# Scatter-add of node features over edges: new places for the steps of the second sort, and one-hots in halves only up to slot 5

## The chip, the cores and the metric

One core of a Trainium2 chip. The metric is device time in microseconds of one execution of the whole program. Three executions of the kernel before were timed, and one more was profiled.

## What is computed

`reference()` adds, for each of 65,536 edges, the 128 features of the source node to the row of the destination node. There are 4,096 nodes, and the edges are drawn at random.

```python
output = np.zeros((num_nodes, dim), dtype=np.float32)
for i in range(len(edge_index_src)):
    output[edge_index_dst[i]] += node_features[edge_index_src[i]]
```

## The kernel before

The features are held as 32 source blocks of 128 rows, and the output is made as 32 destination buckets of 128 nodes. The edges are sorted by destination bucket (the first sort, up to about 50 us), and then, for each of 8 groups of four buckets, by source block (the second sort). What is left is dense work on TensorE (PE): for a source block and a destination bucket, a one-hot of the source rows times a one-hot of the destination columns, both with the edges along the partitions, gives a 128x128 matrix of edge counts (`blocks`, L840, into the PSUM tile `psa`). ScalarE (ACT) copies it to `a`, and `product` (L847) multiplies the block's features by it and adds to `pso`, which holds 512 destinations. Each feature matrix is multiplied in two parts, a rounded one and its remainder.

The main loop (L920) has 32 slots, four for each group, with 8 source blocks in each. For a slot s VectorE (DVE) makes the one-hots of slot s+1 (`onehots`, L825, two instructions of 128x4096 when whole, four of 128x2048 when in halves), and PE does the following: `blocks` of k = 0 to 3 of slot s (16 matmuls), the second half of the products of slot s-1 (8 matmuls), `blocks` of k = 4 to 7 (16), and the first half of the products of slot s (8). The one-hots lie in two buffers, so those of slot s+2 wait for the last `blocks` of slot s. Below, "slot s starts" is the time of the first `psa` matmul of slot s.

The second sort of a group g (`pass2`, L643) has to be done before the one-hots of slot 4g. It is a chain over all engines, and each step is hooked into a place of the loop, written `at(slot, where, step)`. In the order of the code, where 0 is ahead of the one-hots, 1 is right behind them, 2 is ahead of the products of the slot before, 3 and 4 are behind the last `blocks`, and 5 is at the end of the slot. Since the schedule is manual, each engine runs its instructions in exactly the order in which the hooks issue them. The steps are:

- `buckets` (DVE, L662, writes `oh2`), then `chunk_sums` (POOL, L677, writes `two2`, `four2`)
- `payloads` of the group before (POOL, L671, writes `v2`)
- `before_all` (three PE matmuls into `psb`, then ACT writes `base2`, L688), then `masked` and `folded` (POOL, L718 and L724, on `cum2`)
- `repeats` (DVE, L698: a copy and two comparisons into `same2`), then `repeats_folded` (POOL, L713)
- `ranks` (eight PE matmuls into `psr2`, which read `cum2` and `same2`; ACT copies them to `rank2`, L732)
- `permutations` (two instructions of DVE into `p2a` or `p2c`, L745)
- `permuted` (48 PE matmuls into `ps2`, which read `v2`; ACT takes them to `pairs`, L748), then `quad_keys` (two of ACT, L761), which the one-hots of slot 4g read

`two2`, `four2` and `same2` have one buffer each, `oh2`, `cum2` and `v2` two, in turn for even and odd groups. Finished groups go out through `evacuate` (ACT) and `finish` (DVE transpose, L415, then DMAs of the SP queue).

Of the kernel before, what the change touches and what calls it, by code (L numbers as in the profile page):

```python
# [28 lines left out]
GROUPS = (4,) * 8  # L29
WARM = 38  # L30
LATE_PAYLOADS = (2, 3, 4, 5, 6)

TURN = 10
WIN = ((0, 5, 0, 44), (5, TURN, 0, 76), (TURN, 15, 48, 124), (15, NJ, 72, P))
# [45 lines left out]
def _fast(ctx, tc, X, src32, dst32, out, ident, fmax, flag_i, T):  # L80
# [20 lines left out]
    for a, b in runs:  # L101
        at, n = 8 * sum(QN[:a]), 4 * QN[a]
# [152 lines left out]
    def onehot(dst, keys2, n, m=P, io=None, m0=0):  # L255

        io = (piota if io is None else io)[:, None, m0:m0 + m].to_broadcast([P, n, m])
        V.tensor_tensor(  # L258
            out=dst.rearrange("p i (m k) -> p i m k", k=2),
            in0=io.rearrange("p i (m k) -> p i m k", k=2),  # L260
            in1=keys2[:, :, None, :].to_broadcast([P, n, m // 2, 2]), op=OP.is_equal)
# [269 lines left out]
    def pair_onehot(t, r, cs):  # L531
        onehot(t[:, cs].rearrange("p c (u m) -> p (c u) m", u=2)[:, :, :WIDE2],
               r[:, cs].rearrange("p c u k -> p (c u) k"), 2 * (cs.stop - cs.start), WIDE2)
# [13 lines left out]
    def take_pairs(pa, x):  # L547

        x = x.rearrange("p (a j s u) -> p a j s u", a=2, j=2, u=2)
        d = pa.rearrange("p (s j a) -> p a j s", j=2, a=2)  # L550
        S.copy(out=d[:64], in_=x[:64, :, :, :, 0])
        for a in range(2):
            S.copy(out=d[64:, 1 - a], in_=x[64:, a, :, :, 1])
# [9 lines left out]
    def pairs_tile():  # L563
        return sb1.tile([P, 4 * NB], BF16, name="pairs", tag="iota4")
# [68 lines left out]
    owed = {}  # L633
    hooks = {}

    def at(slot, where, *fs):
        hooks.setdefault((slot, where), []).extend(fs)
# [5 lines left out]
    def pass2(g):  # L643
# [101 lines left out]
        def permutations(j):  # L745
            pair_onehot(p2b[d0 // 2 % 4 + j], T2["r"][:, j], slice(0, NCH))

        def permuted(j):  # L748
            if j == 0:
                T2["ps2"] = ps.tile([P, 512], F32, name="ps2", tag="ps2", bufs=1)  # L750
            ps2 = T2["ps2"]
            for c in range(NCH):
                at = (c // NH * 2 + j) * 64
                PE.matmul(out=ps2[:, at:at + 64], lhsT=p2b[d0 // 2 % 4 + j][:, c, :],  # L754
                          rhs=T2["v"][:, c, :, 2 * j:2 * j + 2],
                          start=c % NH == 0, stop=c % NH == NH - 1)
            if j == 1:
                T2["k"] = pairs_tile()
                take_pairs(T2["k"][:], ps2[:, :8 * NB])
# [33 lines left out]
            return lambda: [f() for f in fs]  # L793

        if g == 1:
            at(1, 2, ranks, lambda: permutations(0), lambda: permutations(1))
            at(2, 3, lambda: permuted(0), lambda: permuted(1))
            at(2, 4, quad_keys)
            return buckets, payloads, column_sums, sums_to_each, counts
        if g == 2:  # L800
            owed[2] = payloads
            at(1, 5, before_all, masked, folded)
            at(2, 1, repeats, repeats_folded)
            at(4, 5, ranks)
            at(5, 1, lambda: permutations(0), lambda: permutations(1))
            at(6, 3, lambda: permuted(0), lambda: permuted(1))
            at(6, 5, quad_keys)
            return buckets, chunk_sums
        f = 4 * g
        at(*{3: (3, 1), 4: (6, 1)}.get(g, (f - 11, 4)), buckets, chunk_sums,  # L810
           owed.pop(g - 1, lambda: None))
        after_sums = (5, 5) if g == 3 else (f - 7, 3 if g < 6 else 2)
        at(*after_sums, before_all, masked, folded)
        if g in LATE_PAYLOADS:
            owed[g] = payloads
        else:
            at(*after_sums, payloads)
        at(*((6, 1) if g == 3 else after_sums), repeats, repeats_folded)
        at(f - 4, 3, ranks)
        at(f - 3, 1, lambda: permutations(0), lambda: permutations(1))  # L820
        moves, keys = {3: ((10, 3), (10, 5)), 4: ((14, 2), (14, 5))}.get(g, ((f - 3, 5), (f - 2, 2)))
        at(*moves, lambda: permuted(0), lambda: permuted(1))
        at(*keys, quad_keys)

    def onehots(slot):  # L825

        oh = sb1.tile([P, 2, 4 * 8, P], BF16, name="oh", tag=f"t2{slot % 2}")
        at = slot % 4 * 32
        parts = ((0, 16), (16, 16)) if slot < 9 else ((0, 32),)
        for i, n in ((0, 4), (4, 4), (8, 8), (16, 16)) if slot == 0 else parts:  # L830
            if i == 8 and slot == 0:
                sums_1()
            for k, io in ((0, piota), (1, piotad)):
                onehot(oh[:, k, i:i + n], keys2[slot // 4][k][:, at + i:at + i + n], n, io=io)
        if slot == 0:
            buckets_2()
            chunk_sums_2()
        return oh
# [29 lines left out]
    def flag_of_all(fall):  # L868
# [3 lines left out]
                               op=OP.not_equal)  # L872

    buckets_1, payloads_1, column_sums_1, sums_1, counts_1 = pass2(1)
    buckets_2, chunk_sums_2 = pass2(2)
    for g in range(3, len(GROUPS)):
        pass2(g)
# [37 lines left out]
    counting_1 = counts_1()  # L915
    next(counting_1)
    oh = onehots(0)
    slots = NB
    prev, pso = None, None
    for slot in range(slots):  # L920
        do(slot, 0)
        cur = oh
        if slot + 1 < slots:
            oh = onehots(slot + 1)
# [130 lines left out]
```

## Time and profile before

| what | us |
| --- | --- |
| timed executions | 264.77, 263.05, 264.54 |
| their median | 264.54 |
| profiled execution, device time | 263.02 |
| its span from the first to the last instruction | 261.4 |
| PE busy | 247.2 (95% of the span) |
| DVE busy | 232.5 (89%) |
| ACT busy | 197.0 (75%) |
| POOL busy | 196.8 (75%) |
| mean granted TensorE clock | 0.995 of full speed |

The slices of the page show DVE at 9 tenths and POOL at 9 tenths through most of the first four fifths, and POOL idle from about 209 us on. In the chain of work that ended last PE has 63% and DVE 24%. Times in the rows below are us from the start of the span, and a row with x16 merges 16 instructions; in rows of the timeline the bracket at the end is idle time of that engine before the row and what ended it. Two successive PE rows can overlap by some 0.16 us, since matmuls are pipelined.

### The profile page before, as it was taken

The numbers are of one execution on the slowest core, as the hardware profiler recorded it, in microseconds if no ns is written. First come the engines' busy times: TensorE is split into PE (matmuls) and PEld (weight loads), VectorE is DVE, ScalarE is ACT, GpSimd is POOL, SyncE is SP. The second block draws the span as 40 slices with busy tenths as digits, with TensorE's granted clock in tenths as the row PEclk, the third lists the DMA queues.
The fourth block names the chain that finished last, engine by engine and source line by source line (L and its number), as shares of the span: only waits on it lengthen the run. The fifth ranks groups of instructions, "written<-read, shape, count | busy, mean of one in ns | idle before, by whom it ended". The sixth has DMA issues, their size and how long they took to land.

```text
span 261.4 us, 7518 instructions
## 1 busy us (share of the span) xinstructions
PE 247.2 (95%) x3155; PEld 208.3 (80%) x3156; DVE 232.5 (89%) x245; ACT 197.0 (75%) x455; POOL 196.8 (75%) x211
## 2 busy tenths in 40 slices
PE   7899999899999999899599999999999999999991
PEld 7689999768887888687488877888888888888780
DVE  6998878999999999999999999999999889789701
ACT  5799997698987786678388687687859776887660
POOL 6399999999999999999994999999999900000000
PEclk9999999999999999999999999999999999999998
DMA  5900000000000000220002001100200020002002
GB/s 161 317 8 8 3 4 5 3 0 3 4 0 4 0 3 0 43 40 3 0 0 43 4 1 19 24 3 0 42 1 3 0 44 0 3 1 43 0 1 44
DMA packets 19140, 5.75 MB, mean 22 GB/s; under 512 B 17056, under 2 KB 18592, under 8 KB 19104
## 3 DMA queue, kind: packets, MB, share of 16 engines
q1 hardware_dynamic: 17232, 4.59, 8.0%
q10 hardware_dynamic: 1872, 0.66, 1.2%
q8 instruction: 25, 0.41, 0.6%
q14 instruction: 11, 0.09, 0.1%
HBM read 3.15 MB, written 2.10 MB: 20 GB/s over the span
## 4 chain that ended last, share of the span: by engine, by line
PE 63%; DVE 24%; POOL 4%; issue 4%; ACT 2%; POOLq 0%; DVEq 0%
PE pso L850 33%; DVE oh L258 19%; PE psa L843 16%; PE psm L388 3%; POOL v L363 2%; PE ps L754 2%; PE psc L302 2%; POOL vc L483 2%; PE psw L152 2%; ACT cum L307 1%; DVE p2a L258 1%; DVE p2c L258 1%; PE psc L304 1%; PE pst L280 1%; PE psr L321 1%
## 5 line engine op out<-in xcount | busy, mean ns | idle before, releaser
L845 ACT CAST a<-psa 128x512 fp32r<-128x512 f32 x256 | 131.9, 606 | 36.1 <-PE psa L843 36.0
L850 PE MATMUL pso<-a,xr 128*128 128x512 f32 x512 | 134.0, 404 | 0.0
L850 PEld LDWEIGHTS pso<-a,xr 128*128 128x128 f32 x512 | 91.4, 189 | 16.7
L258 DVE TENSOR_TENSOR oh<-psi,slo 128x4096 bf16<-128x4096 uint16 (+3 forms) x43 | 74.4, 1731 | 3.0 <-PE psa L843 2.1
L258 DVE TENSOR_TENSOR oh<-psi,dlo 128x4096 bf16<-128x4096 uint16 (+3 forms) x43 | 74.5, 1732 | 0.0
L843 PEld LDWEIGHTS <-oh 128*128 128x128 bf16 x1024 | 57.7, 98 | 20.6 <-issue 12.2
L843 PE MATMUL psa<-oh 128*128 128x128 bf16 x1024 | 68.8, 220 | 4.5 <-DVE oh L258 4.5
L721 POOL TENSOR_TENSOR cum<-oh,base 128x512 bf16<-128x512 bf16 x36 | 40.7, 1175 | 4.3 <-ACT base L696 4.2
L674 POOL TENSOR_TENSOR v<-oh,sa 128x512 bf16<-128x512 bf16 x42 | 42.7, 1064 | 0.0
L363 POOL TENSOR_TENSOR v<-oh,kab 128x704 f32<-128x704 bf16 x24 | 32.8, 1411 | 5.2 <-ACT kab L234 5.1
L258 DVE TENSOR_TENSOR p<-psi,rank 128x760 bf16<-128x760 uint16 (+3 forms) x48 | 20.7, 495 | 2.2 <-ACT rank L328 1.2
L685 POOL TENSOR_TENSOR two<-oh 128x512 bf16<-128x512 bf16 x18 | 20.4, 1168 | 0.0
L307 ACT ACTIVATE cum<-psc,sums 128x256 bf16<-128x256 f32 x50 | 19.1, 553 | 0.5 <-PE psc L304 0.5
L388 PE MATMUL psm<-v,p 128*128 128x64 bf16 x512 | 18.2, 193 | 0.0
L388 PEld LDWEIGHTS <-p 128*128 128x128 bf16 x512 | 16.7, 98 | 0.2
L258 DVE TENSOR_TENSOR p2a<-psi,rank 128x2880 bf16<-128x2880 uint16 (+2 forms) x14 | 13.4, 1003 | 0.0
L302 PE MATMUL psc<-early,oh 128*128 128x256 bf16 x67 | 13.2, 272 | 0.0
L258 DVE TENSOR_TENSOR p2c<-psi,rank 128x2880 bf16<-128x2880 uint16 x8 | 12.8, 1642 | 0.0
L665 DVE TENSOR_TENSOR oh<-psi,sbk 128x3072 bf16<-128x3072 uint16 (+1 forms) x8 | 12.3, 1548 | 0.0
L304 PE MATMUL psc<-early,oh 128*128 128x128 bf16 x67 | 12.1, 219 | 0.0
L728 POOL TENSOR_TENSOR cum<-cum 128x384 int32<-128x384 int32 x12 | 11.9, 1020 | 0.0
L685 POOL TENSOR_TENSOR four<-two 128x384 bf16<-128x384 bf16 x12 | 10.8, 928 | 0.0
(123 smaller groups left out, 239.8 us busy)
## 6 DMA issues: line engine op xcount, KB each, us to landing
xf<-in_node_features_dram SPq DMA_DIRECT2D x4, 512.0 KB, 5.7
out_dram<-rows SPq DMA_DIRECT2D x30, 64.0 KB, 2.1
raw<-in_edge_index_src_dram ACTq DMA_DIRECT2D x1, 336.0 KB, 4.7
raw<-in_edge_index_dst_dram SPq DMA_DIRECT2D x1, 336.0 KB, 4.9
raw<-in_edge_index_src_dram ACTq DMA_DIRECT2D x2, 88.0 KB, 2.5
raw<-in_edge_index_dst_dram SPq DMA_DIRECT2D x2, 88.0 KB, 2.6
out_dram<-rows ACTq DMA_DIRECT2D x2, 64.0 KB, 2.9
```

The source lines that it names most:

```text
L258: V.tensor_tensor(out=dst.rearrange("p i (m k) -> p i m k", k=2), in0=io.rearrange("p i (m k) -> p i m k", k=2), in1=keys2[:, :, None, :]. ...
L302: PE.matmul(out=psc[:, at:at + 2 * P], lhsT=oh[:, 2 * i], rhs=early2[:], start=True, stop=False)
L304: PE.matmul(out=psc[:, at + P:at + 2 * P], lhsT=oh[:, 2 * i + 1], rhs=early2[:, :P], start=False, stop=True)
L307: S.activation(out=cum[:, 2 * i:2 * i + 2].rearrange("p j e -> p (j e)"), in_=psc[:, 2 * i * P:2 * (i + 1) * P], func=RELU, bias=bias)
L363: G.tensor_tensor(out=v1[q][:, l::4], in0=oh1q(q)[:, l::4], op=OP.mult, in1=kab[:, q, l::4, None].to_broadcast([P, NJ, NB]))
L388: PE.matmul(out=psm[:, l * 64:(l + 1) * 64], lhsT=t[:, j, l % 2, :], rhs=v1[q][:, 4 * j + l].bitcast(BF16), start=j == 0, stop=j == n - 1)
L674: G.tensor_tensor(out=T2["v"][:, c:c + 4], in0=T2["o"][:, c:c + 4], op=OP.mult, in1=sa[:, c:c + 4, None, d0:d0 + 4].to_broadcast([P, 4, NB ...
L685: G.tensor_tensor(out=to[:, js], in0=of[:, js, 0], in1=of[:, js, 1], op=OP.add)
L721: G.tensor_tensor(out=flat("c")[:, c:c + 4], in0=flat("o")[:, c:c + 4], op=OP.mult, in1=T2["b"][:, c // NH, None].to_broadcast([P, 4, P]))
L843: PE.matmul(out=psa[:, i * P:(i + 1) * P], lhsT=oh[:, 0, 4 * k + i, :], rhs=oh[:, 1, 4 * k + i, :], start=True, stop=True)
L845: S.copy(out=a[:, k, :], in_=psa[:])
L850: PE.matmul(out=pso[:], lhsT=xr[s // 16][:, s % 16, v, :], rhs=a[:, k, :], start=s == 0 and v == 0, stop=s == NB - 1 and v == 1)
```

## The change

A table `PLAN` gives, for the groups 3 to 7, the places of eight steps: `buckets`; `chunk_sums` with the payloads of the group before; `before_all`, `masked` and `folded`; `repeats` with its fold; `ranks`; `permutations`; `permuted`; `quad_keys`. Before, these places came from formulas, and some steps shared one place. Group 2 gets new places for the three steps ahead of its ranks. Besides, the one-hots of the slots 6, 7 and 8 are made whole instead of in halves. No instruction is added or removed but for these: three times four instructions of 128x2048 become two of 128x4096.

```diff
+PLAN = {
+    3: ((2, 2), (4, 1), (6, 2), (4, 5), (8, 0), (9, 1), (10, 3), (11, 0)),
+    4: ((6, 3), (6, 3), (8, 5), (9, 1), (12, 0), (13, 4), (14, 4), (15, 0)),
+    5: ((11, 0), (11, 2), (13, 2), (13, 5), (16, 4), (17, 5), (17, 5), (18, 5)),
...
         if g == 2:
             owed[2] = payloads
-            at(1, 5, before_all, masked, folded)
-            at(2, 1, repeats, repeats_folded)
-            at(4, 5, ranks)
+            at(2, 0, before_all, masked, folded)
+            at(2, 0, repeats, repeats_folded)
+            at(5, 0, ranks)
...
-        at(*{3: (3, 1), 4: (6, 1)}.get(g, (f - 11, 4)), buckets, chunk_sums,
-           owed.pop(g - 1, lambda: None))
-        after_sums = (5, 5) if g == 3 else (f - 7, 3 if g < 6 else 2)
-        at(*after_sums, before_all, masked, folded)
+        first_at, then_at, sums_at, again_at, rank_at, perm_at, move_at, key_at = PLAN[g]
+        at(*first_at, buckets)
+        at(*then_at, chunk_sums, owed.pop(g - 1, lambda: None))
+        at(*sums_at, before_all, masked, folded)
...
-        at(*((6, 1) if g == 3 else after_sums), repeats, repeats_folded)
-        at(f - 4, 3, ranks)
-        at(f - 3, 1, lambda: permutations(0), lambda: permutations(1))
+        at(*again_at, repeats, repeats_folded)
+        at(*rank_at, ranks)
+        at(*perm_at, lambda: permutations(0), lambda: permutations(1))
...
-        parts = ((0, 16), (16, 16)) if slot < 9 else ((0, 32),)
+        parts = ((0, 16), (16, 16)) if slot < 6 else ((0, 32),)
```

Three places show how the instructions move. The first is DVE's queue at the one-hots of slots 10, 11 and 12 (`oh` with `slo2` and `dlo2`; of before `oh_2642`, `oh_2751` and `oh_2876`). Before:

```order
L258 TENSOR_TENSOR oh_2642<-psi_178,slo2_2474 128x4096
L258 TENSOR_TENSOR oh_2642<-psi_178,dlo2_2475 128x4096
L258 TENSOR_TENSOR p2c_1366<-psi_178,rank2_467 128x48x60 x2
L701 COPY psi_178<-sbk_185 128x2x24
L707 TENSOR_TENSOR same2_2721<-psi_178,sbk_185 128x528 x2
L665 TENSOR_TENSOR oh2_2727<-psi_178,sbk_185 128x3072
L258 TENSOR_TENSOR oh_2751<-psi_178,slo2_2474 128x4096
L258 TENSOR_TENSOR oh_2751<-psi_178,dlo2_2475 128x4096
L258 TENSOR_TENSOR oh_2876<-psi_178,slo2_2872 128x4096
```

In the changed kernel the lines of the code stand 7 lower, and the three slots are `oh_2653`, `oh_2729` and `oh_2856`:

```order
L265 TENSOR_TENSOR oh_2653<-psi_178,slo2_2470 128x4096
L265 TENSOR_TENSOR oh_2653<-psi_178,dlo2_2471 128x4096
L265 TENSOR_TENSOR p2c_1366<-psi_178,rank2_467 128x48x60 x2
L708 COPY psi_178<-sbk_185 128x2x24
L714 TENSOR_TENSOR same2_2658<-psi_178,sbk_185 128x528 x2
L265 TENSOR_TENSOR oh_2729<-psi_178,slo2_2470 128x4096
L265 TENSOR_TENSOR oh_2729<-psi_178,dlo2_2471 128x4096
L672 TENSOR_TENSOR oh2_2854<-psi_178,sbk_185 128x3072
L265 TENSOR_TENSOR oh_2856<-psi_178,slo2_2850 128x4096
```

The buckets of group 5 (`oh2`) stand behind the one-hots of slot 11 and no longer ahead of them; the permutations of group 3 (`p2c`) and the repeats of group 4 (`same2`) stay ahead of them.

The second place is DVE's queue at the one-hots of slots 6 and 7 (of before `oh_2240` and `oh_2329`), with the permutations of group 2 (`p2a`). Before:

```order
L258 TENSOR_TENSOR oh_2240<-psi_178,slo2_2058 128x2048
L258 TENSOR_TENSOR oh_2240<-psi_178,dlo2_2059 128x2048
L258 TENSOR_TENSOR oh_2240<-psi_178,slo2_2058 128x2048
L258 TENSOR_TENSOR oh_2240<-psi_178,dlo2_2059 128x2048
L258 TENSOR_TENSOR p2a_117<-psi_178,rank2_467 128x48x60 x2
L258 TENSOR_TENSOR oh_2329<-psi_178,slo2_2058 128x2048
L258 TENSOR_TENSOR oh_2329<-psi_178,dlo2_2059 128x2048
L258 TENSOR_TENSOR oh_2329<-psi_178,slo2_2058 128x2048
L258 TENSOR_TENSOR oh_2329<-psi_178,dlo2_2059 128x2048
L701 COPY psi_178<-sbk_185 128x2x24
L707 TENSOR_TENSOR same2_2334<-psi_178,sbk_185 128x528 x2
L665 TENSOR_TENSOR oh2_2340<-psi_178,sbk_185 128x3072
```

In the changed kernel, with slots 6 and 7 as `oh_2246` and `oh_2316`:

```order
L708 COPY psi_178<-sbk_185 128x2x24
L714 TENSOR_TENSOR same2_2229<-psi_178,sbk_185 128x528 x2
L265 TENSOR_TENSOR oh_2246<-psi_178,slo2_2060 128x4096
L265 TENSOR_TENSOR oh_2246<-psi_178,dlo2_2061 128x4096
L265 TENSOR_TENSOR p2a_117<-psi_178,rank2_467 128x48x60 x2
L265 TENSOR_TENSOR oh_2316<-psi_178,slo2_2060 128x4096
L265 TENSOR_TENSOR oh_2316<-psi_178,dlo2_2061 128x4096
L672 TENSOR_TENSOR oh2_2446<-psi_178,sbk_185 128x3072
```

The repeats of group 3 (`same2`) moved from behind slot 7 to ahead of slot 6, the buckets of group 4 (`oh2`) stay behind slot 7, and each slot has two instructions in place of four. The buckets of group 3, which stood behind slot 4, stand ahead of it now, and the repeats of group 2, which stood behind slot 3, stand ahead of slot 3.

The third place is PE's queue where slot 8 begins: the last products of slot 7 (`pso`), the ranks of group 3 (`psr2`) and the first `blocks` of slot 8 (`psa`). Before, the `blocks` follow on the products, and the ranks come 40 matmuls later, in the middle of the slot:

```order
L843 LDWEIGHTS oh_2329
L843 MATMUL psa_2534<-oh_2329 128x128
L850 MATMUL pso_2162<-a_2483,xr1_183 128x512 x8
L843 LDWEIGHTS oh_2478
L843 MATMUL psa_2559<-oh_2478 128x128
```

In the changed kernel the eight matmuls of the ranks stand between them, and the last of them and what follows are:

```order
L745 LDWEIGHTS identb_89
L745 MATMUL psr2_2548<-same2_2229,identb_89 128x96
L745 LDWEIGHTS identb_89
L745 MATMUL psr2_2548<-same2_2229,identb_89 128x96
L850 LDWEIGHTS oh_2474
L850 MATMUL psa_2564<-oh_2474 128x128
```

The `blocks` of slot 8 are now queued behind the ranks of group 3, and so behind the work of POOL that these read. On POOL itself only the folds of the repeats move: those of group 3 and of group 7 stand ahead of the masked counts of their group instead of behind them.

## Rows read from the trace of the kernel before

**Rows 1.** Windows: busy us of each engine (instructions), PEclk, DMA, GB/s.

```profile
110.00:127.00 17.00, 13.21 (x149) 10.93 (x150) 16.26 (x13) 10.11 (x22) 16.84 (x17) 1.00 0.11 17
127.00:255.60 128.60, 128.56 (x1251) 105.30 (x1251) 112.89 (x71) 96.49 (x204) 77.02 (x78) 1.00 0.07 12
```

**Rows 2.** Chain of waits, in order of time: start us, us, what.

```profile
122.39 4.49 DVE oh L258 x2
...
255.60 0.72 DVE rows L422
```

**Rows 3.** Timeline of PE, slots 4 to 11: start us, us, engine, line, instruction.

```profile
79.08 1.07 PE L843 MATMUL psa<-oh 128*128 128x128 bf16 x16
...
84.71 0.34 PE L738 MATMUL psr<-cum,identb 128*128 128x96 bf16 x4
...
85.06 1.06 PE L843 MATMUL psa<-oh 128*128 128x128 bf16 x16
...
90.67 0.50 PE L694 MATMUL psb<-four,before 128*128 128x256 bf16 x3
91.01 1.06 PE L843 MATMUL psa<-oh 128*128 128x128 bf16 x16
...
94.73 1.60 PE L754 MATMUL ps<-v,p2a 128*128 128x64 bf16 x48
96.17 2.10 PE L850 MATMUL pso<-a,xr 128*128 128x512 f32 x8
98.10 1.07 PE L843 MATMUL psa<-oh 128*128 128x128 bf16 x16
...
103.73 1.07 PE L843 MATMUL psa<-oh 128*128 128x128 bf16 x16
...
110.93 1.07 PE L843 MATMUL psa<-oh 128*128 128x128 bf16 x16 [1.05 <-DVE oh L258]
...
126.92 1.07 PE L843 MATMUL psa<-oh 128*128 128x128 bf16 x16 [2.86 <-DVE oh L258]
```

**Rows 4.** Timeline of DVE, from the permutations of group 1 to slot 12.

```profile
66.89 3.21 DVE L258 TENSOR_TENSOR p2c<-psi,rank 128x2880 bf16<-128x2880 uint16 x2
70.02 1.21 DVE L258 TENSOR_TENSOR oh<-psi,slo 128x2048 bf16<-128x2048 uint16 x1
...
73.41 1.21 DVE L258 TENSOR_TENSOR oh<-psi,dlo 128x2048 bf16<-128x2048 uint16 x1
...
75.59 1.21 DVE L258 TENSOR_TENSOR oh<-psi,slo 128x2048 bf16<-128x2048 uint16 x1
...
80.11 1.75 DVE L665 TENSOR_TENSOR oh<-psi,sbk 128x3072 bf16<-128x3072 uint16 x1
81.78 1.21 DVE L258 TENSOR_TENSOR oh<-psi,slo 128x2048 bf16<-128x2048 uint16 x1
...
111.44 0.72 DVE L415 STREAM_TRANSPOSE rows<-psx 128x512 f32<-128x512 f32 x1 [0.57 <-DMA out_dram<-rows]
...
122.39 2.28 DVE L258 TENSOR_TENSOR oh<-psi,slo 128x4096 bf16<-128x4096 uint16 x1
...
126.79 2.28 DVE L258 TENSOR_TENSOR oh<-psi,slo 128x4096 bf16<-128x4096 uint16 x1
```

**Rows 5.** Timeline of POOL: masked and folded of group 3, then repeats, then sums.

```profile
93.44 6.79 POOL L721 TENSOR_TENSOR cum<-oh,base 128x512 bf16<-128x512 bf16 x6
...
103.88 1.74 POOL L716 TENSOR_TENSOR same<-same 128x480 bf16<-128x480 bf16 x2
105.57 3.41 POOL L685 TENSOR_TENSOR two<-oh 128x512 bf16<-128x512 bf16 x3
...
127.07 1.73 POOL L716 TENSOR_TENSOR same<-same 128x480 bf16<-128x480 bf16 x2
```

**Rows 6.** Timeline of ACT: base of group 3, copies of the first half of slot 6.

```profile
91.21 0.37 ACT L696 CAST base<-psb 128x256 bf16<-128x256 f32 x1 [0.86 <-PE psb L694]
91.49 2.06 ACT L845 CAST a<-psa 128x512 fp32r<-128x512 f32 x4
```

More of the change, by code (lines that the diff above doesn't have):

```diff
@@ L31 @@
 LATE_PAYLOADS = (2, 3, 4, 5, 6)
+PLAN = {
[5 rows of a table added]
+}
 TURN = 10
@@ L795, in pass2 @@
         if g == 1:
-            at(1, 2, ranks, lambda: permutations(0), lambda: permutations(1))
+            at(1, 2, ranks)
+            at(1, 2, lambda: permutations(0), lambda: permutations(1))
             at(2, 3, lambda: permuted(0), lambda: permuted(1))
@@ L816, in pass2 @@
         else:
-            at(*after_sums, payloads)
-        at(*((6, 1) if g == 3 else after_sums), repeats, repeats_folded)
-        at(f - 4, 3, ranks)
-        at(f - 3, 1, lambda: permutations(0), lambda: permutations(1))
-        moves, keys = {3: ((10, 3), (10, 5)), 4: ((14, 2), (14, 5))}.get(g, ((f - 3, 5), (f - 2, 2)))
-        at(*moves, lambda: permuted(0), lambda: permuted(1))
-        at(*keys, quad_keys)
+            at(*sums_at, payloads)
+        at(*again_at, repeats, repeats_folded)
+        at(*rank_at, ranks)
+        at(*perm_at, lambda: permutations(0), lambda: permutations(1))
+        at(*move_at, lambda: permuted(0), lambda: permuted(1))
+        at(*key_at, quad_keys)
     def onehots(slot):
```

2 rows, old and new, of the table PLAN are left out of this document.

## The prediction

> **What bounds the kernel now.** I read the windows first, then the chain of waits, then the timelines of PE, DVE and POOL around the places where the chain changes engine. From 127 us to the last matmul at 255.60 PE is busy 128.56 of 128.60 us, so there the kernel is bound by PE, and nothing that DVE or POOL does sooner can shorten it [rows 1, 2]. The 17 us before that look otherwise: PE is busy 13.21 us of them, DVE 16.26 and POOL 16.84 [rows 1]. PE waits for the one-hots of slot 9 (1.05 us idle) and of slot 11 (2.86 us) [rows 3], and the chain runs through the one-hots made at 122.39 [rows 2]. So 3.9 us are to be had, and they are lost at two places, by DVE being late. After slot 11 DVE pulls ahead.
>
> The reader is to see in DVE's rows why it is late: it has work without a pause up to there. Its only idle time with a cause after slot 2 is 0.57 us for a DMA that frees `rows` [rows 4]. A DVE that never rests finishes the one-hots of slot 11 when all that is queued ahead of them is done, whatever the order. That makes the change easy to cost there: count what leaves the queue ahead of slot 11.
>
> **Durations.** In DVE's queue (start to start) a half instruction takes 1.13 us (70.02 to 73.41 is three), so a slot in halves 4.52; a slot made whole takes 4.40 (122.39 to 126.79); the permutations take 3.13 (66.89 to 70.02), the buckets 1.67 (80.11 to 81.78), and the repeats 1.05 (73.41 + 1.13 = 74.54 to 75.59) [rows 4]. On PE a slot takes 5.63 us (98.10 to 103.73) where nothing else lies in it, and the ranks add 0.35, the `psb` matmuls 0.34 and the permuted ones 1.44 [rows 3].
>
> **What leaves DVE's queue ahead of slot 11.** The buckets of group 5 move behind that slot: 1.67 us. The slots 6, 7 and 8 are made whole: 3 x 0.12 = 0.36. All else that moves (buckets and repeats of group 3, repeats of group 2) moves within the stretch. The one-hots of slot 11 are then done 2.03 us sooner, if DVE meets no new wait: at 122.39 + 4.49 - 2.03 = 124.85 [rows 2].
>
> The 0.12 is where a rule bears on this. The Trainium skill (Perfetto Trace Analysis, section Optimizing Scalar/DVE Operations) gives some 60 ns of fixed cost per DVE instruction on SBUF and advises grouping where the engine is saturated. Two instructions fewer by that figure would be an estimated 0.12 us per slot, and this trace agrees. The same section also says that an engine that is not saturated but causes bubbles elsewhere should break its instructions up; that speaks against the whole one-hots, and it is a rival below.
>
> **Where PE can be by then.** I follow both queues from 66.89, where they are unchanged; a PE start needs the end of the one-hots plus 0.05, and an instruction's end lies 0.08 behind the next one's start.
>
> - Slot 3: the repeats of group 2 now come first, so its first half is ready 1.05 us later, at 73.4, just when PE comes.
> - Slot 4: DVE now makes the buckets of group 3 first. 70.02 + 1.05 + 4.52 + 1.67 = 77.26, first half ready at 77.26 + 2.26 + 0.08 = 79.60. PE would have started at 79.08 [rows 3], now 79.65: a new wait of 0.57.
> - Slot 5: PE 79.65 + 5.63 + 0.35 (ranks of group 2) = 85.63; DVE's half is there at 84.1.
> - The repeats of group 3 gain a wait: `same2` has one buffer, and they must not write it before PE's ranks of group 2 at the head of slot 5 have read it. Those end near 85.8; DVE comes at 77.26 + 2 x 4.52 = 86.30. Nothing is lost, by 0.5 us; all one-hots from slot 6 on are queued behind it.
> - Slot 6, whole: 86.30 + 1.05 + 4.40 = 91.75, ready at 91.88. PE is free at 91.26: a wait of 0.62.
> - Slot 7: PE is free at 91.88 + 5.63 + 0.34 + 1.44 = 99.29 (the `psb` of group 3 now lies in slot 6). DVE: 91.75 + 3.13 + 4.40 = 99.28, ready at 99.41: a wait of 0.12.
> - Slot 8: PE is free at 105.04, DVE is ready at 99.28 + 1.67 + 4.40 + 0.13 = 105.48. But the ranks of group 3 stand at the head of the slot, and they need POOL. POOL is continuous here. With the fold of the repeats (105.57 - 103.88 = 1.69) first, masked and folded (103.88 - 93.44 = 10.44) end at 93.44 + 1.69 + 10.44 = 105.57 as before [rows 5]. The slot starts at 105.57 + 0.1 + 0.35, about 106.05: a new wait of 0.66, on POOL. It holds if the masking can start at 95.13. Its `base2` comes behind ACT's copies of the first four `psa` of slot 6, which end 2.54 us after the slot's start (91.01 to 91.49 + 2.06) [rows 3, 6], so at 94.4, and a copy of 0.37 us later [rows 6] it is there, 0.3 us early.
> - Slot 9: 106.05 + 5.63 + 0.34 = 112.02; slot 10: 117.65; slot 11: 117.65 + 5.63 + 1.44 = 124.72. DVE's 124.85 decides by a hair: PE starts slot 11 at about 124.9 instead of 126.92.
>
> So the waits of 1.05 and 2.86 go and are partly replaced by 0.57, 0.62, 0.12 and 0.66; these lie in slots where PE had time to lose, since slot 11 could not start sooner anyhow. That cover is used up to the last 0.15 us: whatever delays PE more in the slots 8 to 10 costs its full length.
>
> **From slot 11 on.** The buckets of group 5 now delay slot 12: DVE 124.77 + 1.67 + 4.40 + 0.13 = 130.97, PE is free at 124.9 + 5.63 + 0.35 (ranks of group 4, whose folds POOL has at 127.07 + 1.69 = 128.8 [rows 5]) = 130.9, so 0.1 is lost. Group by group the same sums leave PE without a wait: for slots 15 and 16 the one-hots are ready some 0.4 and 0.1 us ahead of PE, and later the lead is a microsecond and more. The remaining steps of groups 6 and 7 (buckets later by a slot, keys later by about a slot) are hidden by that lead and by the fact that a PE slot is 5.63 us and a DVE slot 4.40; without that cover each would cost at most its own 1.67 or about 0.8 us. The moves of the folds on POOL cost nothing, as POOL has no more work than before and ends near 209.
>
> **Sum.** -2.03 at slot 11, +0.1 at slot 12, and about 0.1 back where slot 15 no longer starts with DVE only just done: -2.0 us. Against the profiled execution that is 263.02 - 2.0 = 261.0. The timed runs are 263.05, 264.54 and 264.77, so the profiled one is at their lower end; with it, four executions have the middle 263.8, and I take 261.8 for the median after. Against the median 264.54 alone it would be 262.5. A change of 1% is about what a measurement of this kernel can tell from none, and this is 0.8%.
>
> **Rivals.**
>
> - *The whole one-hots cost what they delay (the rule on breaking up instructions).* In the slots 6 to 8 DVE causes the waits, and half of a one-hot would have let PE start 2.1 us sooner. If the waits at slots 6 and 7 (0.74) are not absorbed before slot 11, the gain is 2.0 - 0.74 = 1.3: 262.5. The sentence of the Trainium skill on breaking instructions up, named above, is the rule behind this. Against it: DVE is saturated here [rows 1], and by the sums above PE waits for POOL at slot 8 and for DVE at slot 11 in any case, and both are reached no sooner with halves.
> - *All waits go.* If POOL and DVE turn out quicker than their rows, the full 3.9 goes: 263.8 - 3.9 = 259.9. Against it: DVE's 2.03 is a count of removed work, and nothing else is removed.
> - *Slower: the ranks at the head of slot 8 wait long.* They stand in PE's queue ahead of `blocks` that are ready. If `base2` of group 3 misses 95.13 (late one-hots of slot 6, or the repeats' wait for `same2`), POOL is late by the same amount for the ranks of group 3 and 4, and PE stands still. PE loses up to 0.15 us free; beyond 0.15 + 2.0 = 2.2 us of lateness the kernel gets slower; at 4.7 late it is 2.5 us slower: 266.3. For it: only 0.3 and 0.5 us of slack on the two conditions. Against it: what could make either late by more than 2 us is not in the trace.
> - *Nothing moves.* Other waits take the whole 2.0, at slots 12 to 16 above all, where the margins are 0.1 to 0.4: 263.8 in the middle, 264.5 by the median. This needs a DVE wait of some 2 us that does not exist before.
>
> **Chances.** The forecast 0.60, the rule on whole one-hots 0.12, all waits go 0.06, nothing moves 0.14, slower 0.08. The range takes the forecast and the two rivals around it, down to 260.2 (261.0 less the 0.8 by which single terms may be off) and up to 264.5 (no change by the median). Faster by over 1% needs 2.65 us and comes from the rival with all waits gone and from the upper edge of the forecast, with the scatter of the runs: 0.27. Slower by over 1% needs 2.2 + 2.65 us of lateness at slot 8: 0.05. The rest is 0.68.
>
> **What would show it.** In the profile after: no idle time of PE ahead of slots 9 and 11 over 0.3 us; the `psa` rows of slot 11 at about 124.9; short waits of PE at slots 4, 6 and 8, the last for POOL; POOL without a pause up to about 140; the last matmul near 253.6. The prediction is wrong if PE waits at slot 8 for more than 0.8 us, if DVE waits at the repeats of group 3, or if PE's waits beyond slot 12 add up to more than half a microsecond.

## The result, and the profile after

| | before | after |
|---|---|---|
| median of 6 executions | 264.43 us (262.88 to 264.77) | 260.31 us (260.24 to 260.50) |
| ratio, 95% interval | | 0.986 (0.983 to 0.989) |
| profiled execution | 263.02 us, span 261.4 | 260.50 us, span 258.8 |

The change makes the kernel 1.4% faster: 4.1 us by the medians, 2.5 us between the two profiled executions. The forecast was 261.8 within 260.2 to 264.5; the time lies in the range, 0.1 us above its low end. Why the two differences are not the same number is the main finding of the experiments.

The windows of the kernel after, first, with the columns of [rows 1] (the second stretch ends with its last matmul, at 252.95; before, that was 255.60):

```profile
110.00:127.00 17.00, 17.00 (x178) 14.09 (x177) 16.86 (x13) 13.57 (x30) 16.84 (x17) 1.00 0.11 16
127.00:252.95 125.95, 125.92 (x1230) 103.24 (x1228) 111.46 (x70) 94.89 (x201) 76.86 (x78) 1.00 0.08 12
```

The 17 us in which PE was busy for 13.21 us [rows 1] now have no hole, and behind them it is busy without a rest as before. The table of waits says what is left of PE's waits between 52 and 254 us (engine, tile, line, what it waited for: us in all, times, longest):

```profile
PE psa L850 <- DVE oh L265: 1.6, 4, 0.6
PE psr L745 <- POOL cum L737: 0.3, 1, 0.3
```

These are idle times; since two successive PE rows else overlap by some 0.16 us, a wait delays the start by that much more. Two of the four waits for one-hots (0.58 us) lie at 52 us, ahead of all that the change touches. The others stand in PE's timeline, at the first `blocks` of slots 4, 6, 7, 8, 9, 11 and 15; the ranks of group 3 stand ahead of slot 8. This answers [rows 3]:

```profile
79.63 1.07 PE L850 MATMUL psa<-oh 128*128 128x128 bf16 x16 [0.40 <-DVE oh L265]
...
91.97 1.07 PE L850 MATMUL psa<-oh 128*128 128x128 bf16 x16 [0.59 <-DVE oh L265]
...
99.50 1.07 PE L850 MATMUL psa<-oh 128*128 128x128 bf16 x16
...
105.59 0.33 PE L745 MATMUL psr<-cum,identb 128*128 128x96 bf16 x4 [0.31 <-POOL cum L737]
105.93 1.06 PE L850 MATMUL psa<-oh 128*128 128x128 bf16 x16
...
111.89 1.06 PE L850 MATMUL psa<-oh 128*128 128x128 bf16 x16
...
124.60 1.07 PE L850 MATMUL psa<-oh 128*128 128x128 bf16 x16
...
149.16 1.07 PE L850 MATMUL psa<-oh 128*128 128x128 bf16 x16
```

| slot | 4 | 5 | 6 | 7 | 8 | 9 | 10 | 11 | 12 |
|---|---|---|---|---|---|---|---|---|---|
| forecast us | 79.65 | 85.63 | 91.88 | 99.41 | 106.05 | 112.02 | 117.65 | 124.9 | 130.97 |
| measured us | 79.63 | 85.61 | 91.97 | 99.50 | 105.93 | 111.89 | 117.50 | 124.60 | 130.58 |

DVE's timeline, to be held against [rows 4]:

```profile
110.42 0.70 DVE L422 STREAM_TRANSPOSE rows<-psx 128x512 f32<-128x512 f32 x1
...
119.66 2.28 DVE L265 TENSOR_TENSOR oh<-psi,slo 128x4096 bf16<-128x4096 uint16 x1
121.86 2.28 DVE L265 TENSOR_TENSOR oh<-psi,dlo 128x4096 bf16<-128x4096 uint16 x1
124.05 1.75 DVE L672 TENSOR_TENSOR oh<-psi,sbk 128x3072 bf16<-128x3072 uint16 x1
```

The one-hots of slot 11 start at 119.66 where they started at 122.39, 2.73 us sooner, and they are done at 124.14, 0.46 us before PE takes them at 124.60. Slot 11 is no longer set by DVE. The transpose at 110.42 has no wait in front of it, where its counterpart had 0.57 us. POOL runs as forecast: the fold of the repeats of group 3 now comes first, and the last step before the ranks ends at 105.54:

```profile
93.41 1.73 POOL L723 TENSOR_TENSOR same<-same 128x480 bf16<-128x480 bf16 x2
95.09 6.77 POOL L728 TENSOR_TENSOR cum<-oh,base 128x512 bf16<-128x512 bf16 x6
...
103.87 1.67 POOL L737 TENSOR_TENSOR cum<-cum 128x384 int32<-128x384 int32 x2
```

### The profile page after: what moved, and what is told of

Read it like the earlier page. It is cut to its first block, busy times and chain, and to the rows that moved or that the text cites. A ratio compares the mean times of both kernels' runs of the same rounds, so it can differ in the third digit from the quotient of the medians.

```text
span 258.8 us, 7508 instructions
## 1 busy us (share of the span) xinstructions
PE 247.1 (95%) x3155; PEld 208.3 (80%) x3156; DVE 231.7 (90%) x239; ACT 197.3 (76%) x455; POOL 196.6 (76%) x211
## 4 chain that ended last, share of the span: by engine, by line
PE 69%; POOL 16%; ACT 9%; DVE 2%; issue 1%; POOLq 0%; DVEq 0%
PE pso L857 37%; PE psa L850 17%; POOL cum L728 5%; ACT cum L314 4%; PE psm L395 3%; PE ps L761 3%; POOL v L681 2%; ACT a L852 2%; PE psw L159 2%; POOL vc L490 2%; POOL cum L735 2%; POOL two L692 1%; POOL same L723 1%; POOL cum L737 1%; PE psc L309 1%; DVE oh L265 1%
## 5 line engine op out<-in xcount | busy, mean ns | idle before, releaser
L723 POOL TENSOR_TENSOR same<-same 128x480 bf16<-128x480 bf16 (+1 forms) x12 | 9.9, 825 | 6.2 <-DVE same L714 5.7
```

## The experiments

**1. The kernel before, once more.** No edit. Its executions spread over 2 us and those of the kernel after over 0.3 us, so the spread itself needs a reason. Theory A: DMA traffic. Theory B: TensorE's clock.

> The kernel before, unchanged, for a second profile and more timed executions. Six timed executions of it lie at 262.9 to 263.1 (two) and 264.4 to 264.8 (four), while all six of the changed kernel lie within 0.3 us. Theory A (the extra 1.5 us is DVE's lateness ahead of slot 11 that grows when a store's DMA lands late): the clock is the same in all executions, and a profile at 264.5 would show a longer wait of DVE for the DMA that frees the tile rows than the 0.57 us of the first profile, with PE's wait at slot 11 grown by as much. Theory B (the granted clock falls in PE's waits at slots 9 and 11): the executions at 264.5 show a mean clock lower by about 0.01 than those at 263. By both, the times fall into the same two heaps again.

Measured: median 264.37 us over 10 executions, 262.94 to 265.91. All executions of this kernel in the four batches of experiments, 78 of them, lie in three clusters, called heaps here, with nothing between, and each heap has its own mean granted clock:

| us | executions | mean granted clock |
|---|---|---|
| 262.85 to 263.09 | 29 | 0.994 to 0.996 |
| 264.09 to 264.87 | 43 | 0.987 to 0.990 |
| 265.64 to 266.04 | 6 | 0.984 |

The execution profiled here was one of the slowest, 265.91. Two windows of the profile ahead of the prediction (263.02), then those of this one, and its timeline of PE from slot 11:

```profile
124.00:127.00 3.00, 0.14 (x3) 0.08 (x3) 3.00 (x3) 0.00 (x0) 2.84 (x4) 1.00 0.00 0
127.00:133.00 6.00, 6.00 (x56) 4.93 (x57) 6.00 (x3) 4.12 (x9) 5.92 (x8) 1.00 0.00 0
```

```profile
124.00:127.00 3.00, 0.07 (x2) 0.05 (x2) 3.00 (x3) 0.00 (x0) 2.84 (x4) 0.86 0.00 0
127.00:133.00 6.00, 6.00 (x32) 4.90 (x33) 4.29 (x2) 2.20 (x5) 5.92 (x8) 0.50 0.00 0
133.00:141.00 8.00, 8.00 (x74) 6.68 (x72) 6.51 (x4) 6.58 (x15) 6.85 (x7) 1.00 0.05 9
```

```profile
126.95 1.89 PE L843 MATMUL psa<-oh 128*128 128x128 bf16 x16 [2.93 <-DVE oh L258]
128.60 3.76 PE L850 MATMUL pso<-a,xr 128*128 128x512 f32 x8
132.17 1.46 PE L843 MATMUL psa<-oh 128*128 128x128 bf16 x16
133.44 2.09 PE L850 MATMUL pso<-a,xr 128*128 128x512 f32 x8
```

While PE waits 2.93 us for the one-hots of slot 11, the granted clock falls (0.86 is a mean over the stretch), and the first 6 us of work after it run at 0.50, which is 1.2 of 2.4 GHz: eight `pso` matmuls take 3.76 us in place of 2.09. Slot 12 starts 8.4 us after slot 11 (at 135.37) and not 5.63, and those 2.8 us are the distance of the third heap from the first. The DMA wait of `rows` was 0.6 us as in the other profile. Theory B holds and A falls. The profile ahead of the prediction showed an execution of the first heap, at 1.00 in and behind the same wait, so the wait of 2.86 us in [rows 3] has a further price that its rows don't show.

The Trainium skill (TensorE: Matmul & The Clock Gate, section What's actually happening) says that the clock has two levels, set by recent activity, and that the watch does not begin anew with a kernel, so that the moment of a change differs from run to run. The levels 1.00 and 0.50 here, and one program with three times, agree.

**2. Matmuls in the wait.** The kernel before, with 45 dummy matmuls put on PE ahead of slot 11, whose products nobody reads. They remove no wait of the data, only PE's rest.

```
     column_sums_1()
+    at(10, 5, lambda: keep_busy(45))
     counting_1 = counts_1()
```

> The kernel before, with 45 matmuls of 128 columns on a tile that nobody reads put into PE's wait ahead of slot 11 (2.86 us of idle time there, 45 of them take about 2.6 us); nothing else. Theory B (in the second profile of the kernel before the granted clock is 0.50 from 127 to 133 us, right behind this wait): with PE at work in the wait the clock stays at 1.00 there, all executions fall into the lower heap, 262.9 to 263.1, and none lies at 264.2 to 266. Theory A or any other cause of the upper heap: executions above 264 remain. By either no execution is faster than 262.8, since slot 11 still waits for DVE.

Measured: 263.02 us median of 12 executions, 262.87 to 263.31, all at clock 0.993 or more; of 17 executions of the kernel before in the same batch 8 lay at 264.38 to 264.86. Its windows:

```profile
124.00:127.00 3.00, 2.56 (x46) 2.38 (x43) 3.00 (x2) 0.00 (x0) 2.84 (x4) 1.00 0.00 0
127.00:133.00 6.00, 5.85 (x52) 4.80 (x53) 6.00 (x4) 4.11 (x8) 5.92 (x8) 1.00 0.01 3
```

PE is busy in the former wait, ACT is still idle there (0.00), slot 11 still waits for DVE, and the clock stays at 1.00. So the upper two heaps need PE's rest: with it filled, none of 12 executions lies in them. Why some executions keep the clock through the same rest is not shown. In this batch the median of before was 263.09, as 9 of the 17 lay in the first heap, so the ratio is only 0.997 (0.995 to 0.999); against the 264.43 of the result it is 1.4 us. That is about what lies between the 4.1 us of the medians and the 2.6 us between the first heap and the kernel after (262.9 to 260.3).

**3. The rows' DMA wait.** The kernel before, with a transpose and store of finished rows at the end of slot 6 too and not only from slot 7 on, which takes away the 0.57 us that DVE waited for the single `rows` buffer [rows 4].

```
-        if not 4 <= slot < 7:
+        if not 4 <= slot < 6:
             finish()
```

> The kernel before with the first finished group transposed and stored one slot sooner, in slot 6, so that the transpose in slot 8 does not wait for the DMA that frees rows. Theory: DVE loses its 0.57 us wait ahead of slot 11; slot 8 starts some 0.5 us later, which slot 9's wait takes up; the time is 263.0 - 0.5 = 262.5. If late landings of that DMA are what makes the executions at 264.5 (theory A of the run of the kernel before), all executions lie within 0.5 us of each other, near 262.5. If it is the clock (theory B), they still fall into two heaps 1.5 us apart.

Measured: 262.99 us median of 10, ratio 0.996 (0.993 to 1.000), still in two heaps: 262.12 to 262.24 (clock 0.995, 0.996) and 263.73 to 263.88 (0.988, 0.989). The lower heap lies 0.7 us below that of the kernel before, so this wait was worth about its length. Theory A is out here too, as the upper heap stays with the wait gone. The profiled execution is of the upper heap:

```profile
126.08 1.28 PE L843 MATMUL psa<-oh 128*128 128x128 bf16 x16 [2.18 <-DVE oh L258]
127.12 3.51 PE L850 MATMUL pso<-a,xr 128*128 128x512 f32 x8
```

```profile
122.00:126.00 4.00, 1.90 (x8) 1.21 (x7) 4.00 (x3) 1.62 (x5) 3.92 (x5) 1.00 0.00 0
126.00:130.40 4.40, 4.32 (x24) 3.50 (x24) 4.40 (x3) 2.05 (x4) 4.24 (x6) 0.61 0.00 0
```

After a wait of 2.18 us the clock can still fall, here only when PE is at work again (1.00 up to 126, 0.61 in the mean of the 4.4 us behind it). The drop cost 1.6 us: slot 12 starts 7.2 us after slot 11 and not 5.63.

**4. Only the buckets of group 5 later.** The kernel before with one part of the change: the buckets behind the one-hots of slot 11, their sums two places later.

```
-        at(*{3: (3, 1), 4: (6, 1)}.get(g, (f - 11, 4)), buckets, chunk_sums,
+        at(*{3: (3, 1), 4: (6, 1), 5: (11, 0)}.get(g, (f - 11, 4)), buckets)
+        at(*{3: (3, 1), 4: (6, 1), 5: (11, 2)}.get(g, (f - 11, 4)), chunk_sums,
```

> The kernel before with one step moved: the buckets of group 5 from behind slot 10's one-hots to behind slot 11's, with the chunk sums and the payloads of group 4 a little later. Theory (DVE's queue is counted): slot 11 starts 1.66 us sooner, at 125.3, the idle time of 1.05 at slot 9 stays, and the profiled time is 263.0 - 1.6 = 261.4. Rival (the gain comes from the plan as a whole, since slot 12 is then late by the same step): slot 12 takes the wait, and the time stays at 263.0.

Measured: 262.35 us median of 10, 262.21 to 262.57, ratio 0.994 (0.991 to 0.997), one heap. PE's waits from slot 9 on, at slots 9, 11, 12 and 15:

```profile
110.94 1.07 PE L844 MATMUL psa<-oh 128*128 128x128 bf16 x16 [1.03 <-DVE oh L258]
125.41 1.07 PE L844 MATMUL psa<-oh 128*128 128x128 bf16 x16 [1.32 <-DVE oh L258]
131.47 1.07 PE L844 MATMUL psa<-oh 128*128 128x128 bf16 x16 [0.28 <-DVE oh L258]
151.20 1.07 PE L844 MATMUL psa<-oh 128*128 128x128 bf16 x16 [0.63 <-DVE oh L258]
```

Slot 11 comes 1.51 us sooner, as a bucket's length says, but at slot 15 (151.20, before 151.66) only 0.46 us is left. The buckets now stand ahead of slot 12, and ahead of slot 15 the queue holds as much work as before, so the lead is taken back there. What is left is about a wait of DVE for ACT that the kernel before has between the two slots and this one has not (its transpose starts at 135.73 without one):

```profile
136.17 0.72 DVE L415 STREAM_TRANSPOSE rows<-psx 128x512 f32<-128x512 f32 x1 [0.51 <-ACT psx L401]
```

So the truth lies between the two expectations: 0.6 us below the heap at 262.9, where 1.6 and nothing were expected. The wait of 1.32 us at slot 11 brings no drop of the clock in ten executions.

**5. The buckets of group 5 put back.** The kernel after, with this one place as it was.

```
-    5: ((11, 0), (11, 2), (13, 2), (13, 5), (16, 4), (17, 5), (17, 5), (18, 5)),
+    5: ((9, 4), (9, 4), (13, 2), (13, 5), (16, 4), (17, 5), (17, 5), (18, 5)),
```

> The changed kernel with the buckets of group 5 (and its chunk sums) back at their old place, ahead of slot 11's one-hots. Theory: DVE has the one-hots of slot 11 ready at 124.14 + 1.67 = 125.81, PE starts slot 11 at 125.87 in place of 124.60, and the time is 260.5 + 1.3 = 261.8. Rival (these buckets do not matter in the new plan): 260.5.

Measured: 261.56 us median of 6, 261.46 to 261.75, ratio to before 0.991 (0.988 to 0.993): 1.25 us of the gain go.

```profile
125.87 1.07 PE L850 MATMUL psa<-oh 128*128 128x128 bf16 x16 [1.05 <-DVE oh L265]
```

Slot 11 starts 1.27 us later: the 1.67 of the buckets less the 0.46 that DVE is ahead there now make 1.21.

**6. The buckets of group 6 put back.** The kernel after, with `(14, 4)` in group 6 as `(13, 4)`, which puts the buckets ahead of slot 15 again.

```
-    6: ((14, 4), (16, 2), (17, 1), (18, 1), (20, 0), (20, 4), (21, 5), (23, 0)),
+    6: ((13, 4), (16, 2), (17, 1), (18, 1), (20, 0), (20, 4), (21, 5), (23, 0)),
```

> The changed kernel with the buckets of group 6 back ahead of the one-hots of slot 15 (their chunk sums stay). Theory (DVE's queue ahead of slot 4g-1 decides in each group, not at slot 11 alone): the one-hots of slot 15 are ready at 148.24 + 1.67 = 149.91, 0.75 behind PE's 149.16, and nothing makes that up later: 260.3 + 0.8 = 261.1. Rival (after slot 11 DVE is far enough ahead): 260.3.

Measured: 261.06 us median of 4, 260.96 to 261.30: 0.75 us of the gain go. Slot 15 stands at 149.94 in place of 149.16:

```profile
149.94 1.07 PE L850 MATMUL psa<-oh 128*128 128x128 bf16 x16 [0.53 <-DVE oh L265]
```

So the gain at slot 11 reaches the end in full only because the next group's buckets were moved as well. The prediction counted that step among those "hidden by that lead".

**7. The whole one-hots undone.** The kernel after, with halves up to slot 8 as before. This is the rival of the rule on breaking instructions up.

```
-        parts = ((0, 16), (16, 16)) if slot < 6 else ((0, 32),)
+        parts = ((0, 16), (16, 16)) if slot < 9 else ((0, 32),)
```

> The changed kernel with the one-hots of the slots 6, 7 and 8 in halves again, as before. Forecast (the waits of PE at slots 6 and 7 are covered, since slot 8 waits for POOL's folds of group 3 in any case): PE's waits of 0.59 at slot 6 and 0.03 at slot 7 go, its wait for POOL at slot 8 grows from 0.31 to about 1.1, slot 8 starts at 105.9 again, and the time is the same within 0.2 us: 260.3 to 260.5. Rival (whole one-hots cost what they delay): 0.6 to 0.7 us faster, 259.7.

Measured: 260.34 us median of 6, 260.31 to 260.48, against 260.31 with whole ones: no difference. PE's waits:

```profile
PE psr L745 <- POOL cum L737: 1.2, 1, 1.2
PE psa L850 <- DVE oh L265: 1.0, 3, 0.4
```

The wait of 0.59 us at slot 6 is gone with halves. The Trainium skill (Perfetto Trace Analysis, section Optimizing Scalar/DVE Operations) gives the advice to break instructions up for an engine that causes bubbles without being saturated; DVE is saturated here (busy for 16.86 of 17.00 us in the window shown for the kernel after), and the bubble went all the same. But PE then stands at the ranks of group 3 for 1.2 us in place of 0.3, since POOL is no sooner. Slot 11 is at 124.43 in place of 124.60, and 0.15 us of that this execution has from its first slot on (51.86 in place of 52.01). Neither form is worth anything over the other here; the rival falls for the reason that the prediction gave.

**8. Only the whole one-hots.** The kernel before, with the other part of the change alone.

```
-        parts = ((0, 16), (16, 16)) if slot < 9 else ((0, 32),)
+        parts = ((0, 16), (16, 16)) if slot < 6 else ((0, 32),)
```

> The kernel before with the other part of the change alone: the one-hots of the slots 6, 7 and 8 whole, all places as before. Forecast: DVE saves 0.36 us ahead of slot 11, PE waits some 0.3 us at slot 7 and 1.4 us at slot 8, these waits take the place of the one at slot 9, and slot 11 starts at about 126.6 in place of 126.92: 262.6 for executions with the clock at 1.00. Rival (whole one-hots cost what they delay): 1 us or more slower. PE's wait ahead of slot 11 is still some 2.1 us, so executions with the halved clock should still be there, if such a wait is what brings it down.

Measured: 261.82 us median of 8, 261.77 to 262.07, one heap, clock 0.993 to 0.997; ratio 0.992 (0.989 to 0.995). Slots 8 and 11 are where PE waits:

```profile
105.65 1.07 PE L843 MATMUL psa<-oh 128*128 128x128 bf16 x16 [1.40 <-DVE oh L258]
...
125.98 1.07 PE L843 MATMUL psa<-oh 128*128 128x128 bf16 x16 [1.23 <-DVE oh L258]
```

Slot 11 comes 0.94 us sooner. That is the 0.36 us of six instructions fewer and the 0.57 us of the rows' DMA wait, which is not among the waits any more. Against the heap at 262.9 it is 1.1 us, and the higher heaps are gone on top. The wait of 1.4 us at slot 8 was expected. The rest of the expectation (slot 11 at 126.6, a wait of 2.1 us ahead of it) failed, as it kept the DMA wait. The wait at slot 11 is 1.23 us, because DVE is sooner and because PE comes to it later (slot 10 starts at 117.50, before at 116.81). With waits of 1.40 and 1.23 us no execution has the lower clock. So the whole one-hots, which cost nothing and bring nothing in the changed kernel, would have been worth over a microsecond alone: the parts of the change do not add up.

**9. A third plan.** The kernel after with places of its own: each DVE step stands behind the one-hots of every slot that can be served ahead of it, and halves stand only where PE would wait for them (slots 0 to 3, 5, 9, 11, 13). Two lines of the table, and the halves; group 2 and groups 4, 6 and 7 move by similar steps:

```
-    3: ((2, 2), (4, 1), (6, 2), (4, 5), (8, 0), (9, 1), (10, 3), (11, 0)),
+    3: ((3, 4), (5, 3), (6, 0), (6, 5), (9, 3), (10, 0), (10, 3), (10, 3)),
-    5: ((11, 0), (11, 2), (13, 2), (13, 5), (16, 4), (17, 5), (17, 5), (18, 5)),
+    5: ((11, 1), (12, 3), (14, 2), (14, 4), (16, 5), (17, 4), (18, 4), (19, 0)),
+HALVES = [0, 1, 2, 3, 5, 9, 11, 13]
```

> The changed kernel with a third set of places, worked out with the durations of the changed kernel's rows so that PE never waits between slot 2 and slot 29: buckets of groups 3 to 7 at slots 3, 7, 11, 15 and 19 behind the one-hots, repeats one to two slots after them, ranks behind the first half of a slot or later, and one-hots in halves for the slots 1, 2, 3, 5, 9, 11 and 13 alone. PE's waits in the changed kernel at slots 4 (0.40), 6 (0.59), 7 (0.03) and 8 (0.31) of idle time, 1.6 us with what each costs at its start, go: 260.3 - 1.6 = 258.7. If DVE or POOL is the bound of the whole loop rather than these waits, the time stays at 260.3.

Measured: 260.36 us median of 6, 260.29 to 260.44: as the kernel after, not 258.7. One wait of PE took nearly all of it:

```profile
115.07 0.50 PE L702 MATMUL psb<-four,before 128*128 128x256 bf16 x3 [1.45 <-ACT rank L750]
```

At place (9, 3) the plan put both the ranks of group 3 and the `psb` matmuls of group 4 (`before_all`). Their PSUM tiles share one buffer, so the second waits until ACT has copied the first, and ACT has the copies of `psa` queued ahead.

**10. The two apart.** The third plan with the ranks of group 3 a slot sooner.

```
-    3: ((3, 4), (5, 3), (6, 0), (6, 5), (9, 3), (10, 0), (10, 3), (10, 3)),
+    3: ((3, 4), (5, 3), (6, 0), (6, 5), (8, 3), (10, 0), (10, 3), (10, 3)),
```

> The third set of places with one step moved: the ranks of group 3 in slot 8 instead of slot 9, where they shared a place with the psb matmuls of group 4. In the run before, PE waited 1.5 us there, for ACT to copy the ranks out of the one PSUM buffer that psr2, psb2 and ps2 share. Theory (that buffer alone ate the gain): the wait goes, every slot from 10 on starts 1.5 us sooner, and the time is 260.36 - 1.5 = 258.9. Rival (DVE or POOL is the bound of the loop): the time stays near 260.3.

Measured: 259.83 us median of 6, 259.70 to 260.06, not 258.9. The buffer's wait is gone, and another stands behind it: PE at slot 10, and ahead of it DVE's transpose.

```profile
116.50 1.07 PE L851 MATMUL psa<-oh 128*128 128x128 bf16 x16 [0.68 <-DVE oh L266]
```

```profile
111.35 0.72 DVE L423 STREAM_TRANSPOSE rows<-psx 128x512 f32<-128x512 f32 x1 [0.92 <-ACT a L853]
```

The row names ACT, but the tile that the transpose reads had been copied at 107.39; so it must have lacked the `rows` buffer, which the store of the rows before had still to leave; the last of that store landed at 111.23. It is the wait of [rows 4] again.

**11. The store later.** The kernel of experiment 10, with no store at the end of slot 8; its rows go out a slot later, with the next.

```
-        if not 4 <= slot < 7:
+        if not 4 <= slot < 7 and slot != 8:
             finish()
```

> The third set of places with the ranks in slot 8, and the transpose of the second finished group one slot later (slot 9 instead of 8). In the run before, DVE's one-hots of slot 10 started 0.92 us late: the transpose ahead of them had to wait until the store of the first group had left rows, whose last landing came at 111.23, 1.8 us after the others, with one 16 KB packet of the instruction queue on the DMA engines at 109.1. Theory (that store ate 0.7 us, PE's idle time at slot 10): with the transpose behind slot 10's one-hots the wait of PE at slot 10 goes, and the time is 259.8 - 0.6 = 259.2. Rival (DVE's own work is the bound there): the lost time shows up at slots 12, 14 and 15 instead, and the time stays at 259.8.

Measured: 258.71 us median of 5, 258.66 to 258.82, ratio to before 0.979 (0.977 to 0.981): 1.6 us below the kernel after, and the best of all. Against experiment 10 it is 1.1 us, where 0.6 was expected; slot 11 starts 0.8 us sooner (122.79, there 123.59), and the rest comes at later slots. Its last matmul ends at 251.40. Between 52 and 252 us PE's waits are now these, both at 52 us, and its windows show no rest behind them:

```profile
PE psa L851 <- DVE oh L266: 0.6, 2, 0.3
```

```profile
52.00:110.00 58.00, 57.66 (x606) 47.23 (x607) 57.79 (x50) 47.96 (x100) 57.39 (x58) 1.00 0.04 6
110.00:127.00 17.00, 17.00 (x189) 14.29 (x187) 17.00 (x12) 13.13 (x28) 16.84 (x17) 1.00 0.11 17
```

## Why the prediction was right, and where it was wrong

**The mechanism was right.** PE waited at slots 9 and 11 because a DVE that never rests was late, and the slot-by-slot working of both queues came out within 0.15 us up to slot 10. The new waits stand where they were forecast (0.40, 0.59 and 0.31 us at slots 4, 6 and 8; forecast 0.57, 0.62 and 0.66), the one at slot 8 for POOL. DVE had no wait at the repeats of group 3, so the slower rival did not come about. The term of the buckets is confirmed by experiment 5, and that halves would reach slot 11 no sooner by experiment 7; so the 0.36 us of the whole one-hots in the sum is worth nothing beside the other moves. The rival "all waits go" (259.9) lies nearer to the time than the forecast does, but not for its reason: the new waits are there, and what the forecast missed is mostly the price of the clock, below.

**The new waits were not free.** The prediction put them in slots "where PE had time to lose". Those at slots 6 and 7 cost nothing, as PE would have stood at slot 8 for POOL (experiment 7). But DVE had the one-hots of slot 11 ready 0.46 us ahead of PE, so PE's own line, with the wait for POOL in it, was the later one. A plan without these waits comes to 1.6 us less, once the waits that stood behind them are gone too (experiments 9 to 11).

**The baseline was wrong, and this is the largest miss.** The step was: "four executions have the middle 263.8, and I take 261.8 for the median after". It took the spread from 263.05 to 264.77 for scatter that the kernel after would have too. It is the price of the wait itself: 49 of 78 executions lie in the two heaps with the lower mean clock, 1.5 or 2.8 us up, and in the profile of one of them the granted clock falls to 0.50 at PE's rest ahead of slot 11. A change that takes the rest away moves all executions into the heap below: all six after lie within 0.3 us. Set right, the sum of -2.0 would start from the heap at 262.9 and give about 260.9 us for every execution, 3.5 us under the median of before. So the statement that 1% is what a measurement tells, and the chance of 0.27 for faster by over 1%, both came from the same mistake. That the range held all the same is luck: its low end, 260.2, was 0.8 us below the 261.0 of the profiled execution, and 0.8 us below the forecast of 261.8 it would have ended at 261.0. The signs were there: one profile at the low end of the times, at clock 0.995, and two of three timed executions 1.5 us above it.

**The rows' DMA wait was counted as staying.** The step "if DVE meets no new wait" thought of waits that come and took the 0.57 us of [rows 4] as one that stays. It went. In the kernel before one packet of 16 KB on the instruction queue starts at 108.6 us, amid the store's packets, and the last of these run until 110.6; in the kernel after the store's packets are through at 109.3, and that packet starts at 109.7. The stores issued between 106 and 112 us (queue, issues, KB each, median us to landing), before and after:

```profile
out_dram<-rows SPq DMA_DIRECT2D x4, 64.0 KB, 2.7
```

```profile
out_dram<-rows SPq DMA_DIRECT2D x6, 64.0 KB, 2.0
```

The medians hide the piece that counts: of the first four issues the slowest takes 3.5 us before, and 2.0 us after. So DVE was 2.73 us sooner at slot 11 and not 2.03. Only 0.3 us of that could be used, as the start of slot 11 was then set by PE's own line (forecast 124.72, measured 124.60), which the prediction had 0.13 us ahead of DVE's.

**The terms behind slot 11 came to nothing in the sum and were 0.3 us.** The 0.1 us lost at slot 12 did not occur, since DVE was ahead. Slot 15 starts at 149.16 against 151.66, a gain of 2.50 us where slot 11 had 2.32; slots 19 and 31 have 2.62 and 2.64, and the last matmul ends at 252.95 against 255.60, a gain of 2.65 (forecast: near 253.6). The prediction read from [rows 1] that behind 127 us nothing DVE does sooner can help. But before, DVE set the start of slots 15 and 19 too: its one-hots end there at 151.60 and 176.32, and PE takes them at 151.66 and 176.38. That is no idle time, only the 0.16 us by which successive rows else overlap; the gain grows by 0.18 us at slot 15 and by 0.12 us up to slot 19. For slot 15, before:

```profile
151.66 1.07 PE L843 MATMUL psa<-oh 128*128 128x128 bf16 x16
```

The sum was -2.0; the difference is -2.5 between the profiled executions and -2.6 from the first heap to the kernel after.

**One thing was right by the plan and not by the argument.** The prediction treated the buckets of group 6 as hidden in any case. Experiment 6 shows 0.75 us on them, and experiment 4 shows that the buckets of group 5 alone bring about 0.5 us and not 1.7: what is moved behind one slot is late for the next that asks, until a slot comes whose queue has room.

Not settled is why the drop of the clock lasts for 1.5 us of lost time in most of the executions that have it, and for 2.8 in a few.

## What to carry to other kernels

When an engine never rests, count what stands in its queue ahead of the instruction that is waited for, and repeat the count at the next such points: a gain at one of them reaches the end only if the later ones have room too, and a shared buffer or a store can be the next thing late. Before taking spread in the times of a kernel for noise, put each execution's granted clock beside its time: heaps with a clock of their own can mean, as here, that a wait has a second price, and a change that shortens this wait is then worth more than its length.

## What the runs showed of the hardware

- A rest of PE of 2.9 us in the middle of steady work can let the granted clock fall from 1.00 to 0.50: by their times and mean clocks in 49 of 78 executions, at a cost of 1.5 or 2.8 us; with one of 2.2 us it did so in 5 of 10. One profile of each kind shows the fall itself. After rests of 1.0 to 1.5 us (experiments 4, 5, 8 and 9, 30 executions) none showed it. Dummy matmuls in the rest of 2.9 us kept the clock at 1.00 in 12 of 12.
- A finished group is stored by four issues of 64 KB. For the first such store of the loop, seven of the 13 profiles (those of both kernels and of the eleven experiments) show every issue landing within 2.0 us; in these the 16 KB packet of the instruction queue starts behind all of the store's packets. In the other six it starts ahead of the last of them, and the slowest issue takes 3.5 to 4.2 us. With one buffer for the rows, that was 0.57 us of DVE's time in the kernel before, and 0.92 us in experiment 10. That the instruction packet is the cause was not tested by itself; moving the store took the wait away in experiments 3 and 11.
